# Holding one stream's expert row fetches back to the later long convolutions of a hybrid layer

## The chip, the cores and the metric

The kernel runs on one core of a Trainium2 chip. The metric is device time in microseconds (us), from the start to the end of one execution. The core has five engines that run their own instruction lists in order and wait for each other through semaphores: TensorE (PE in the profile), VectorE (DVE), ScalarE (ACT), GpSimd (POOL) and SyncE (SP), and 16 DMA engines that all of them can give transfers to.

## What is computed

One layer of a model runs over two groups of tokens, a prompt of 256 tokens (stream P) and a sample of 1024 tokens (stream Q), with the same weights. Cut to what matters here:

```python
def trunk_layer(x, cond, h0, p):
    y, final_state = token_mixer(x * (1 + sc1) + sh1, h0, p)   # projection, RG-LRU scans, long convolutions
    x = layer_norm(ALPHA * x + g1 * y, ...)
    y = peer(x * (1 + sc2) + sh2, ...)                         # 8 heads x top 16 of 16384 experts
    x = layer_norm(ALPHA * x + g2 * y, ...)

def peer_block(xb):                       # 128 tokens
    idx, g = route(xb)                    # 128 expert numbers and weights per token
    u = u_tab[idx]                        # one row of 1024 floats per token and expert
    act = gelu(einsum("td,thkd->thk", xb, u))
    v = v_tab[idx]
    return einsum("thk,thkd->td", g * act, v)

def hyena_branch(hy):                     # two rounds of FFT convolution over the whole sequence
    z = x1 * fft_long_conv(v, kf[:, 0], skip[0])
    z = x2 * fft_long_conv(z, kf[:, 1], skip[1])
```

## The kernel before

**The experts of stream P as row fetches.** `experts` (its helper `fetch` stands at L1046) handles a block of 128 tokens with 128 fetches from the u table and then 128 from the v table. A fetch is one indirect DMA that GpSimd issues: 128 rows of 1024 floats, one row per token, 0.52 MB. VectorE then takes the row tile: L1059 multiplies a u row with the token's vector and sums (the vector `h` lies in PSUM), L1068 adds a weighted v row to the sum. Both keep VectorE busy for one instruction per fetch. Five row buffers (`row`, `bufs=5`) go round, so a sixth fetch waits on GpSimd until VectorE has taken the first. P has two blocks, so 512 fetches, numbered 0 to 511 by `fetched`; numbers 256 to 383 are the u rows of the second block. They are filler beside the mixer of stream Q.

**Where they may run.** `PACE["P"]` is a list of (number, mark): a fetch may not stand on GpSimd ahead of the mark of the last entry whose number is not above its own (`paced`). A mark is a GpSimd instruction of stream Q that `mark` noted; `"hy"` counts 32 of them, the products L721 at the end of each long convolution. `_pace(first, (name, start, stop, each), ...)` gives the numbers: each mark lets `each` more fetches through. Fetches ahead of the first number have no mark and go as soon as buffers and GpSimd allow. The rest of the order of all engines is set by the framework's scheduler, which reorders within the dependences.

**The long convolutions of stream Q.** `hyena` runs eight convolutions, two rounds (`o`) over four groups of 256 channels, in pairs: groups 0 and 1 in round 0, then in round 1, then groups 2 and 3. One convolution (`convolve`) is

- folds of the input (L341) and their splits into high and low parts (`oph`, `opl`, L204, L205), on VectorE and GpSimd;
- the analysis: TensorE multiplies the folds with cosine and sine tables for four blocks of frequencies, into two PSUM banks each (L162);
- on VectorE the products with the filter's spectrum (L703, L704, L705, `ya`, `yb`, `k`) and their split (`yh`, `yl`);
- the synthesis: TensorE multiplies `yh` and `yl` back to time, 192 matmuls into four banks, a quarter of them with the last frequency block;
- VectorE takes the four banks in two pairs of sums (L720, `z`), and GpSimd multiplies each by the gate `x` (L721). These four are four `"hy"` marks.

In this text "the first pair" and "the second pair" of a convolution are its L720 instructions, two and two. The numbers 1 to 8 name the convolutions in order. What follows them is branch A and B (`branch`): ScalarE's queue loads the results of the scans and of the convolutions (`z<-d_ZAQ`, `z<-d_ZBQ`, L794), they are split, and the products with `w_branch_a` start.

Of the kernel before, what the change touches and what calls it, by code (L numbers as in the profile page):

```python
# [20 lines left out]
P = 128  # L21
# [31 lines left out]
def _pace(first, *segments):  # L53

    out = []
    for name, start, stop, each in segments:
        for i in range(start, stop):
            out.append((int(first), (name, i)))
            first += each
    return out  # L60
# [1 line left out]

SCANS = (10, 14, 18, 22, 26, 30, 34, 38, 41)
ORDER = (0, 1, 5, 2, 3, 4, 6, 7)
PACE = {"P": _pace(340, ("hy", 0, 32, 0.5), ("w_branch_a", 0, 8, 4), ("w_branch_b", 0, 8, 4), ("w_out", 0, 16, 2), ("query", 0, 32, 2)),
        "Q": _pace(0, ("spread", 16, 80, 3))}


# [32 lines left out]
def body(ctx, tc, A, O):  # L101
# [88 lines left out]
    def paced(pace, i, ins):  # L190

        at = [m for first, m in pace if first <= i]
        if at:
            tc.add_manual_dep(ins.ins, marks[at[-1]].name, mybir.DependencyInfo(mybir.DependencyClass.NoSync, mybir.DependencyReason.DATA), reason="pace")
# [844 lines left out]
    def experts(s, blocks, out, peer, ready=None):  # L1039

        for b in blocks:
            idx, g = s.route[b]

            def fetch(tab, k):
                t = row(peer)
                i = nc.gpsimd.indirect_dma_start(out=t[:], out_offset=None, in_=A[tab],  # L1046
                                                 in_offset=bass.IndirectOffsetOnAxis(ap=idx[:, k:k + 1], axis=0))
                paced(PACE[s.name], fetched[s.name], i)
                fetched[s.name] += 1
# [405 lines left out]
```

## Time and profile before

| | us |
|---|---|
| median of 3 runs (5077.14 to 5094.96) | 5087.09 |
| the profiled execution, its own time | 5079.36 |
| its span | 5077.6 |
| TensorE busy | 4316.5 (85%) |
| VectorE busy | 4128.4 (81%) |
| GpSimd busy | 3045.0 (60%) |
| ScalarE busy | 1821.2 (36%) |

Shares are means over stages with different limits. The projection of stream Q runs until about 1685 us, the eight convolutions from 1697 to about 2140, the branches, output, norm and queries until about 2600, the routing and the spreading of the experts' weights until about 3400, then the dense experts until 4925 and the last row fetches of stream Q to the end. A row of a busy-time view gives a stretch, its length, the busy time of each engine with the number of instructions, the clock that TensorE was granted as a share of 2.4 GHz, the mean busy share of the DMA engines and their GB/s. A row of a timeline gives start, length, engine, line, operation and, in square brackets, how long the engine sat idle before it and what ended that.

### The profile page before, as it was taken

Reading aid. Unit: us, or ns where it says so; the run is one execution under the profiler, and the core shown is the slowest. Engines: PE = TensorE matmul, PEld = TensorE weight load, DVE = VectorE, ACT = ScalarE, POOL = GpSimd, SP = SyncE. Lnnn points to the kernel's source line nnn. Section 1 sums busy time; section 2 is a strip of 40 time slices with the busy share of each in tenths; the row PEclk is TensorE's granted clock in tenths of the full one; section 3 lists DMA queues with packets and bytes.
Section 4 is the critical chain, followed back from the end, with each engine's and each line's share of the span. In section 5 each row is a group of like instructions: output and inputs, shape, how many; then the busy total and the mean of one; then the engine's idle time right before and its main releaser. Section 6 shows DMA issues by size and latency. Waiting matters only on the chain.

```text
span 5077.6 us, 67877 instructions
## 1 busy us (share of the span) xinstructions
PE 4316.5 (85%) x23707; PEld 3762.4 (74%) x23707; DVE 4128.4 (81%) x7106; ACT 1821.2 (36%) x2716; POOL 3045.0 (60%) x2218
## 2 busy tenths in 40 slices
PE   6888788899999678789798888888699999999970
PEld 4666687677777668767587888888588888888860
DVE  6779563989994877466759999999589899989898
ACT  4546333346663112121433544445232222222210
POOL 1456451478886765368664365667467676666765
PEclk8999899999999889999899999999899999999995
DMA  6676646798889853388685478887988999989988
GB/s 210 219 237 201 194 159 220 245 325 305 299 302 328 300 177 119 127 319 300 246 290 180 158 240 281 282 282 261 342 302 327 343 334 340 330 311 338 339 285 296
DMA packets 613378, 1357.26 MB, mean 267 GB/s; under 512 B 64254, under 2 KB 284103, under 8 KB 612524
## 3 DMA queue, kind: packets, MB, share of 16 engines
q1 hardware_dynamic: 417196, 658.69, 38.5%
q0 software_dynamic: 187776, 680.61, 38.0%
q10 hardware_dynamic: 8064, 13.64, 0.7%
q8 instruction: 186, 3.05, 0.2%
q14 instruction: 156, 1.28, 0.1%
HBM read 1182.81 MB, written 169.93 MB: 266 GB/s over the span
## 4 chain that ended last, share of the span: by engine, by line
PE 22%; DVE 16%; issue 7%; DMA 7%; POOL 4%; SPq 2%; ACT 1%; POOLq 0%; ACTq 0%; DVEq 0%
PE bank L162 18%; PE bank L171 3%; DVE row L1059 3%; DVE oa L1098 2%; POOL row L1046 2%; DMA row<-in_peer_v,idxQ 2%; SPq L1104 2%; DVE y L1068 2%; DVE ob L1095 1%; DVE hot L1090 1%; DVE gt L1151 1%; PE bank L1101 1%; DMA row<-in_peer_u,idxQ 1%; DVE S L931 1%; DVE iu L930 1%
## 5 line engine op out<-in xcount | busy, mean ns | idle before, releaser
L1068 DVE SCALAR_TENSOR_TENSOR y<-row,act,y 128x1024 f32<-128x1024 f32 x635 | 815.7, 1285 | 199.6 <-DMA row<-in_peer_v,idxP 112.6
L1059 DVE SCALAR_TENSOR_TENSOR row<-row,h 128x1024 f32<-128x1024 f32 x640 | 763.2, 1212 | 131.7 <-DMA row<-in_peer_u,idxP 67.5
L162 PE MATMUL bank<-hTh,uh 128*128 128x320 f32 x2048 | 646.5, 316 | 46.0 <-ACT uh L204 45.9
L162 PE MATMUL bank<-hTl,uh 128*128 128x320 f32 x2048 | 645.3, 315 | 0.0
L162 PE MATMUL bank<-hTh,ul 128*128 128x320 f32 x2048 | 643.5, 315 | 1.8 <-POOL ul L205 1.8
L1046 POOL DMA_INDIRECT row<-in_peer_u,idxQ x384 | 411.5, 1072 | 293.7 <-DVE row L1059 187.2
L1046 POOL DMA_INDIRECT row<-in_peer_v,idxQ x384 | 411.6, 1072 | 270.5 <-DVE y L1068 202.1
L205 POOL TENSOR_TENSOR wl<-wr,wh 128x1024 fp32r<-128x1024 f32 x148 | 364.3, 2462 | 331.9 <-ACT wh L204 303.9
L162 PE MATMUL bank<-vl,wh 128*128 128x512 f32 x1280 | 497.5, 390 | 3.8 <-DVE vl L205 3.5
L162 PE MATMUL bank<-vh,wh 128*128 128x512 f32 x1280 | 489.2, 392 | 13.0 <-ACT wh L204 7.2
L162 PE MATMUL bank<-vh,wl 128*128 128x512 f32 x1280 | 482.9, 390 | 0.8 <-DVE wl L205 0.6
L162 PEld LDWEIGHTS bank<-hTh,uh 128*128 128x128 f32 x2048 | 394.3, 193 | 48.6 <-ACT uh L204 47.3
L162 PEld LDWEIGHTS bank<-hTl,uh 128*128 128x128 f32 x2048 | 394.4, 193 | 1.2
L162 PEld LDWEIGHTS bank<-hTh,ul 128*128 128x128 f32 x2048 | 393.0, 192 | 2.7 <-POOL ul L205 2.6
L1046 POOL DMA_INDIRECT row<-in_peer_u,idxP x256 | 275.0, 1074 | 142.4 <-DVE row L1059 79.4
L204 ACT ACTIVATE wh<-wr 128x1024 fp32r<-128x1024 f32 x176 | 185.7, 1057 | 443.2 <-issue 171.6
L1046 POOL DMA_INDIRECT row<-in_peer_v,idxP x256 | 277.3, 1083 | 102.3 <-issue 35.6
L205 POOL TENSOR_TENSOR ul<-raw,uh 128x1024 fp32r<-128x1024 f32 x100 | 242.8, 2428 | 111.6 <-ACT uh L204 110.1
L1101 PE MATMUL bank<-ob,oa 128*128 128x128 f32 x1280 | 190.7, 302 | 125.5 <-DVE oa L1098 74.4
L162 PEld LDWEIGHTS bank<-vh,wh 128*128 128x128 f32 x1280 | 240.9, 188 | 67.9 <-ACT wh L204 9.7
L162 PEld LDWEIGHTS bank<-vl,wh 128*128 128x128 f32 x1280 | 240.7, 188 | 53.7 <-DVE vl L205 4.4
L162 PEld LDWEIGHTS bank<-vh,wl 128*128 128x128 f32 x1280 | 240.7, 188 | 52.4 <-DVE wl L205 1.5
(444 smaller groups left out, 12046.6 us busy)
## 6 DMA issues: line engine op xcount, KB each, us to landing
raw<-in_peer_uT SPq DMA_DIRECT2D x128, 512.0 KB
raw<-in_peer_v SPq DMA_DIRECT2D x128, 512.0 KB
wr<-in_w_in SPq DMA_DIRECT2D x112, 512.0 KB
d_GD<-G SPq DMA_DIRECT2D x40, 1024.0 KB
gt<-d_GD SPq DMA_DIRECT2D x128, 320.0 KB
w<-in_w_ada SPq DMA_DIRECT2D x48, 512.0 KB
wr<-in_w_query SPq DMA_DIRECT2D x48, 512.0 KB
d_AD<-a SPq DMA_DIRECT2D x72, 320.0 KB
```

The source lines that it names most:

```text
L162: nc.tensor.matmul(out, l, r, start=(i == 0), stop=(i == len(ops) - 1))
L171: nc.tensor.matmul(out, a, b, start=(i + j == 0), stop=(i == KT - 1 and j == len(ops) - 1))
L204: nc.scalar.activation(hi, src, AF.Copy)
L205: note(eng, eng.tensor_tensor(lo, src, hi.bitcast(F32), op=ALU.subtract))
L930: nc.vector.max_index(iu[:, g, 0:8], v[:, g, 0:8], Sg)
L931: nc.vector.match_replace(S2[:], v[:, g, 0:8], Sg, NEG)
L1046: i = nc.gpsimd.indirect_dma_start(out=t[:], out_offset=None, in_=A[tab], in_offset=bass.IndirectOffsetOnAxis(ap=idx[:, k:k + 1], axis=0))
L1059: nc.vector.scalar_tensor_tensor(t[:], t[:], 1.0, h[:], op0=ALU.mult, op1=ALU.mult, accum_out=act[:, k:k + 1])
L1068: nc.vector.scalar_tensor_tensor(y[:], t[:], act[:, k:k + 1], y[:], op0=ALU.mult, op1=ALU.add)
L1098: nc.vector.tensor_scalar(oa[:, i, :], iota_k[:], tr[:, 0, t:t + 1], tr[:, 2, t:t + 1], op0=ALU.is_equal, op1=ALU.mult)
L1101: nc.tensor.matmul(ps[:, i * P:(i + 1) * P], oa[:, i, :], ob[:, i, :], start=True, stop=True)
L1104: nc.sync.dma_start(GD[j:j + 16, :, b * P:(b + 1) * P].rearrange("j i t -> i j t"), G[:, j:j + 16, :])
```

## The change

`PACE["P"]` gets two other numbers and one more segment:

```diff
-PACE = {"P": _pace(340, ("hy", 0, 32, 0.5), ("w_branch_a", 0, 8, 4), ...
+PACE = {"P": _pace(292, ("hy", 0, 12, 0.5), ("hy", 12, 32, 3), ("w_branch_a", 0, 8, 4), ...
```

Before, fetches 0 to 339 are free and 340 to 355 go one for every two marks of the convolutions. Now 0 to 291 are free, 292 to 297 go one for every two of the marks 0 to 11, and 298 to 357 three for each of the marks 12 to 31. The segments behind follow as they did, with numbers that are two higher (358 stands where 356 stood). No instruction is added or removed.

The instruction lists of the two kernels differ as follows. On VectorE at the end of convolution 1 (`row,act<-row,h` is the taking of a u row, `z<-bank_14370` and `z<-bank_14488` are the two pairs of convolution 1, `ya` and `yb` with bank 14654 and 14667 belong to convolution 2):

```order
-L1059 SCALAR_TENSOR_TENSOR row,act<-row,h 128x1024 x2
+L720 TENSOR_TENSOR z<-bank_14370,ya 128x512 x2
+L720 TENSOR_TENSOR z<-bank_14488,ya 128x512 x2
+L1059 SCALAR_TENSOR_TENSOR row,act<-row,h 128x1024
+L703 TENSOR_TENSOR ya<-bank_14654,k_14680 128x512
+L703 TENSOR_TENSOR ya<-bank_14654,k_14682 128x512
 L704 TENSOR_TENSOR yb<-bank_14667,k_14682 128x512
-L1059 SCALAR_TENSOR_TENSOR row,act<-row,h 128x1024 x3
-L720 TENSOR_TENSOR z<-bank_14370,ya 128x512 x2
```

The rows that stood ahead of the first pair are gone from there. Counted over the whole list, 23 fewer rows stand ahead of the first pair of convolution 1, and 25 fewer between it and the first pair of convolution 2 (2 where there were 27).

On VectorE between convolutions 4 and 5 (bank 15916 and 16026 are the two pairs of convolution 4, and what follows is the analysis of convolution 5):

```order
 L720 TENSOR_TENSOR z<-bank_15916,ya 128x512 x2
+L1059 SCALAR_TENSOR_TENSOR row,act<-row,h 128x1024
 L720 TENSOR_TENSOR z<-bank_16026,ya 128x512 x2
-L1059 SCALAR_TENSOR_TENSOR row,act<-row,h 128x1024
+L1059 SCALAR_TENSOR_TENSOR row,act<-row,h 128x1024 x2
 L704 TENSOR_TENSOR yb<-bank_16257,k_16272 128x512
-L205 TENSOR_TENSOR opl<-fold,oph 128x512
+L205 TENSOR_TENSOR opl<-fold,oph 128x512 x2
+L1059 SCALAR_TENSOR_TENSOR row,act<-row,h 128x1024
```

One row now stands between the two pairs and eleven behind them, in the first half of the next analysis, where there were none and two. It is the same in front of convolutions 6, 7 and 8. Behind convolution 8's second pair 11 rows now stand ahead of the splits of the branch, where there was one.

On GpSimd at the end of convolution 4 (`z<-z,x` is a mark, `row<-in_peer_u` a fetch):

```order
-L721 TENSOR_TENSOR z<-z,x 128x512 x2
-L1046 DMA row<-in_peer_u,idxP_9588 128x1024
-L721 TENSOR_TENSOR z<-z,x 128x512 x2
-L1046 DMA row<-in_peer_u,idxP_9588 128x1024
+L721 TENSOR_TENSOR z<-z,x 128x512
+L1046 DMA row<-in_peer_u,idxP_9588 128x1024 x3
+L721 TENSOR_TENSOR z<-z,x 128x512
+L1046 DMA row<-in_peer_u,idxP_9588 128x1024 x3
+L721 TENSOR_TENSOR z<-z,x 128x512 x2
+L1046 DMA row<-in_peer_u,idxP_9588 128x1024 x2
```

Three fetches stand behind each of the first two marks, and the six of the other two are mixed with the folds and splits that follow.

## Rows read from the trace of the kernel before

**Rows 1.** Page, part 1: busy time, share of the span, instructions.

```profile
PE 4316.5 (85%) x23707; PEld 3762.4 (74%) x23707; DVE 4128.4 (81%) x7106; ACT 1821.2 (36%) x2716; POOL 3045.0 (60%) x2218
```

**Rows 2.** Busy times: from first pair to first pair of the convolutions, and behind.

```profile
core 0: us, PE busy (x) PEld busy (x) DVE busy (x) ACT busy (x) POOL busy (x), PEclk, DMA share, GB/s
1697.00:1775.00 78.00, 52.05 (x353) 49.42 (x354) 74.82 (x113) 15.34 (x26) 59.22 (x52) 0.78 0.87 291
1775.00:1843.00 68.00, 42.95 (x275) 40.08 (x275) 62.55 (x93) 10.13 (x17) 46.59 (x41) 0.77 0.72 250
1843.00:1897.00 54.00, 45.48 (x346) 43.63 (x346) 38.65 (x49) 11.05 (x19) 30.25 (x21) 0.91 0.32 102
1897.00:1942.00 45.00, 40.78 (x329) 40.12 (x328) 27.98 (x40) 10.43 (x17) 24.52 (x18) 0.96 0.32 101
1942.00:1989.00 47.00, 43.45 (x358) 43.01 (x357) 30.63 (x41) 14.93 (x42) 22.89 (x17) 0.96 0.39 129
1989.00:2040.00 51.00, 45.73 (x371) 44.84 (x370) 34.97 (x44) 11.88 (x26) 26.29 (x19) 0.93 0.31 99
2040.00:2088.00 48.00, 40.11 (x316) 39.16 (x315) 33.59 (x42) 10.80 (x19) 26.94 (x19) 0.93 0.29 94
2088.00:2127.00 39.00, 39.00 (x334) 39.00 (x333) 23.27 (x35) 6.25 (x10) 15.86 (x12) 1.00 0.27 82
2127.00:2175.00 48.00, 20.77 (x118) 16.23 (x116) 11.85 (x16) 18.81 (x55) 18.75 (x14) 0.72 0.86 304
```

**Rows 3.** The same for line 1059 alone (two records for each row taken).

```profile
1775.00:1843.00 68.00, 32.52 (x54) 0.77 0.72 250
1942.00:1989.00 47.00, 2.46 (x4) 0.96 0.39 129
```

**Rows 4.** Line 1059 from 1690 to 2140: shortest, median, longest in ns.

```profile
L1059 DVE SCALAR_TENSOR_TENSOR row<-row,h x76: 1203/1211/1223, 1692.1 to 2135.2; 128x1024 f32<-128x1024 f32 x76
```

**Rows 5.** VectorE's timeline at the ends of convolutions 1, 2 and 4 to 8.

```profile
1774.77 1.29 DVE L720 TENSOR_TENSOR z<-bank,ya 128x512 f32<-128x512 f32 x2
...
1844.63 1.29 DVE L720 TENSOR_TENSOR z<-bank,ya 128x512 f32<-128x512 f32 x2 [5.67 <-PE bank L162]
...
1853.92 1.22 DVE L1059 SCALAR_TENSOR_TENSOR row<-row,h 128x1024 f32<-128x1024 f32 x1 [4.66 <-DMA row<-in_peer_u,idxP]
...
1855.07 1.28 DVE L720 TENSOR_TENSOR z<-bank,ya 128x512 f32<-128x512 f32 x2
...
1941.95 1.29 DVE L720 TENSOR_TENSOR z<-bank,ya 128x512 f32<-128x512 f32 x2 [8.48 <-ACT ya L715]
1948.90 1.29 DVE L720 TENSOR_TENSOR z<-bank,ya 128x512 f32<-128x512 f32 x2 [5.66 <-ACT ya L715]
...
1989.45 1.29 DVE L720 TENSOR_TENSOR z<-bank,ya 128x512 f32<-128x512 f32 x2 [9.34 <-PE bank L162]
...
2040.16 1.29 DVE L720 TENSOR_TENSOR z<-bank,ya 128x512 f32<-128x512 f32 x2 [8.36 <-ACT ya L715]
...
2088.01 1.29 DVE L720 TENSOR_TENSOR z<-bank,ya 128x512 f32<-128x512 f32 x2 [7.41 <-ACT ya L715]
...
2126.76 1.29 DVE L720 TENSOR_TENSOR z<-bank,ya 128x512 f32<-128x512 f32 x2 [5.92 <-ACT ya L715]
```

**Rows 6.** GpSimd's timeline behind the first pair of convolution 2.

```profile
1845.40 2.54 POOL L721 TENSOR_TENSOR z<-z,x 128x512 f32<-128x512 f32 x2 [9.06 <-DVE z L720]
1848.09 1.42 POOL L1046 DMA_INDIRECT row<-in_peer_u,idxP  x1 [0.15 <-issue]
```

**Rows 7.** The chain that ended last, behind the convolutions: start, us, what.

```profile
2170.33 12.13 DMA z<-d_ZBQ
```

**Rows 8.** TensorE's timeline: matmuls at the higher and at the lower clock.

```profile
1942.47 0.28 PE L162 MATMUL bank<-yh,kN 128*128 128x256 f32 x1
1942.59 0.28 PE L162 MATMUL bank<-yl,kN 128*128 128x256 f32 x1
...
1974.62 0.41 PE L162 MATMUL bank<-yh,kN 128*128 128x256 f32 x1
1974.84 0.41 PE L162 MATMUL bank<-yl,kN 128*128 128x256 f32 x1
```

**Rows 9.** Busy times of the stage of routing and spreading.

```profile
2600.00:3400.00 800.00, 683.45 (x4358) 649.10 (x4357) 766.61 (x2427) 356.48 (x450) 448.59 (x314) 0.94 0.72 237
```

More of the change, by code (lines that the diff above doesn't have):

```diff
@@ L64 @@
 ORDER = (0, 1, 5, 2, 3, 4, 6, 7)
-PACE = {"P": _pace(340, ("hy", 0, 32, 0.5), ("w_branch_a", 0, 8, 4), ("w_branch_b", 0, 8, 4), ("w_out", 0, 16, 2), ("query", 0, 32, 2)),
+PACE = {"P": _pace(292, ("hy", 0, 12, 0.5), ("hy", 12, 32, 3), ("w_branch_a", 0, 8, 4), ("w_branch_b", 0, 8, 4), ("w_out", 0, 16, 2), ("query", 0, 32, 2)),
         "Q": _pace(0, ("spread", 16, 80, 3))}
```

## The prediction, made before the changed kernel ran

> **What bounds the kernel now.** I read the page's busy shares first: TensorE 85% and VectorE 81% [rows 1], so neither alone explains the span, and each stage has to be read by itself. All that the change moves lies in one stage, so next comes the view of busy time cut at the first pair of each long convolution [rows 2]. The reader is to see two kinds of stretch. In the first two (78 and 68 us) VectorE is idle for only 3.2 and 5.5 us and TensorE is granted 0.78 and 0.77 of its clock: VectorE is the bound. In the six others VectorE is idle 14 to 17 us each, and the clock is 0.91 to 1.00. The same view for line 1059 alone [rows 3] says what fills the first kind: 27 rows take 32.5 us of the second stretch, while a later stretch has 2 rows. A row costs 1.21 us whatever runs beside it, 1203 to 1223 ns over 76 of them [rows 4].
>
> Then VectorE's timeline [rows 5] shows where the idle time of a later convolution lies: 5.9 to 9.3 us ahead of the first pair and some 5.7 us between the pairs, while TensorE finishes the synthesis. The analysis between them is one unbroken run of VectorE work. So a row costs nothing in the end of a synthesis and its full price in an analysis. Everything behind the convolutions needs their output, and the later stages keep their work, so a shift of their end should pass to the end of the program.
>
> **Part 1, rows taken out of convolutions 1 and 2.** 23 rows fewer stand ahead of the first pair of convolution 1: 23 x 1.21 = 27.8 us of VectorE. That pair, at 1774.77, waited for nothing [rows 5]; without filler a wait for TensorE comes back, 5.7 to 9.3 us. I take 7: gain 20.8. Convolution 2 loses 25 rows, 30.3 us; its idle time grows from 5.5 us to the 15.6 us that is the mean of the stretches of 5 to 8 (16.4, 16.0, 14.4, 15.7 [rows 2]): gain 20.2. Its second pair also waited behind a row whose transfer had not landed, and came 10.44 us after the first, against 6.95 in convolution 4 [rows 5]. That gives up to 3.5 us; some other work was done in that gap, so I take 2. Sum of part 1: 43 us. The ends: 60 if no wait comes back, 39 if the longest does and the last gain is nothing.
>
> **Part 2, rows put ahead of convolutions 5 to 8.** Each now gets 12 rows instead of 2. The order shows where: one between the pairs, eleven behind them, in the first half of the next analysis, where VectorE has no gap. That is 9 rows more at 1.21 = 10.9 us in the run that sets the pace. The row between the pairs is not free either: its fetch is issued behind the first mark. In convolution 2 the fetch stood behind two marks and the second pair came 10.44 us after the first; one mark is half of 2.54 us [rows 6], so now it comes 10.44 - 1.27 = 9.2 us after, 2.2 later than the 6.95 of a pair without a row. Sum per convolution 13.1, for four 52.4. Some comes back: TensorE has work in hand when the analysis ends, so the wait ahead of the first pair can shrink, at best to the 5.67 us of the loaded convolution 2, from 9.34, 8.36, 7.41 and 5.92 [rows 5]: 8.3 us in all. Since the rows stand in the first half, and TensorE meets an unchanged second half, I take half of it: 4.2. Part 2 costs 48 us. The ends: if the gaps shrink to the 5.5 us of the loaded convolution 2, 10.1 of 12.1 us is hidden each time and four cost 8 us; at full price and with the clock of the rival below, 71.
>
> **Part 3, rows behind convolution 8.** Eleven rows stand there where one stood; 10 more fetches of 0.52 MB are 5.2 MB. The chain there is the loading of the branch's operands, a 12.1 us stretch of it among others [rows 7], and the DMA engines are 86% busy at 304 GB/s [rows 2], so 5.2 MB at 304/0.86 = 353 GB/s take 14.8 us. About half of the fetches are issued ahead of the last marks, when the engines have room. I take half, 7.4, between 0 (all land ahead of the loads) and 14.8. The Trainium skill, "DMA: Bandwidth & Descriptors", section on issuing engines not being separate queues, says that transfers of every issuing queue run on the same 16 engines and interleave; no row here shows a fetch beside these loads, and by that rule alone the term would be its upper end and the sum 7 us more. VectorE's eleven rows are no term of their own: VectorE is idle there for 36 of 48 us [rows 2].
>
> **Part 4, two rows fewer later.** P's fetches end two earlier, in a stage where VectorE is busy 767 of 800 us [rows 9]: 2 x 1.21 = 2.4 us gained, or nothing. GpSimd's own issue work is the same in total; it is hidden since GpSimd is at most 60% busy in the later stretches [rows 2].
>
> **Sum.** -43 + 48 + 7.4 - 2.4 = +10 us on the profiled execution's 5079.4 us, 5089 us. The median of the runs lies 7.7 us above that execution, so I put the forecast at 5087 + 10 = 5097 us: the saving of the first two convolutions is given back in the last four, and a bit more at the branch.
>
> **Rivals.** First, faster: the rows find the gaps. In convolution 2, 27 rows left only 5.5 us idle, so VectorE can be packed when rows are at hand. For it speaks that each later stretch has 14 to 17 us free for 12.1 us of new work; against it, that in convolution 2 rows went whenever a buffer came free, and here they come in bursts behind the marks, into the busy half. Part 2 is then 8: -43 + 8 + 7 - 2 = -30, 5057 us.
>
> Second, slower: TensorE's clock falls in convolutions 5 to 8. The mechanism is one: the eleven rows make TensorE wait for VectorE in every analysis, the granted clock drops as in convolutions 1 and 2 (0.77), and the last quarter of the synthesis, 48 matmuls that need the last product, runs at the lower level. Matmuls start 0.12 us apart at the higher and 0.22 at the lower level [rows 8], so 48 of them take 4.6 us longer, 18 us for four convolutions, and no wait shrinks. Part 2 is then 71 and, with the branch's upper end, the sum is -43 + 71 + 15 - 2 = +41, 5128 us. It decides from about 1.3 us per convolution on, since the forecast is only 5 us below the bound of slower. For it speaks that the lower level already appears inside convolution 5 [rows 8]; against it, that this stretch kept 0.96 [rows 2]. The Trainium skill, "TensorE: Matmul & The Clock Gate", section on HAM oscillation, says that a wait which returns in every pass of a loop throttles the clock in every pass. By that rule this rival is the forecast; the trace agrees in convolutions 1 and 2 and not yet in the later ones.
>
> Third, the change does nothing: the end of the convolutions is not what the branch waits for, since its weights and loads bound it anyway. Then 5087 us. Against it: the chain runs through the last marks and the loads behind them.
>
> **How the numbers follow.** About 0.3% (15 us) is what a measurement of this kernel can tell from no change. The forecast has 0.38 and the third rival 0.06, both within the bound: same 0.44. The faster rival has 0.20, the slower 0.36, because the forecast stands near the upper bound and its two unproven terms (clock, loads) both point up. The likeliest case alone reaches from 5083 (more of the wait shrinks, no price at the branch) to 5110. The range for 8 in 10 takes in both rivals' sides, 5058 to 5126.
>
> **What would show it.** Cut at the first pairs, convolution 1's end should come 21 us earlier after its start, convolution 2 should last about 48 us, and 5 to 8 about 59, 63, 60 and 51, each 12 us longer. If those last four grow by 5 us or less, the first rival holds; if the granted clock there falls below 0.9, the second. The second pair of convolutions 4 to 7 should come some 9 us after the first, behind a row that waited for its transfer. The time from the last mark to the first steady products of branch A should grow by 0 to 15 us. The forecast is wrong if the later stages differ by more than their start, since the order of routing and spreading moved a little too.

## The result and the profile after

The changed kernel takes 5131.2 us (median of 6 runs, 5123.1 to 5134.7); the kernel before, beside it, 5081.4. The ratio is 1.0093, with a 95% interval of 1.0081 to 1.0105: some 47 us slower. By the medians it is 49.8 us. The forecast was 5097 (5058 to 5126): the trade between the convolutions came out nearly as forecast, the end did not. The profiled execution of after took 5124.3 us, its span is 5122.4, 44.8 us more than that of before.

Page, part 1, of after (against [rows 1]):

```profile
PE 4342.7 (85%) x23707; PEld 3789.0 (74%) x23707; DVE 4126.2 (81%) x7106; ACT 1821.3 (36%) x2716; POOL 3050.1 (60%) x2218
```

The instructions are the same; TensorE's 26 us more go with a mean granted clock of 0.919 against 0.926. Next the busy times of after, cut at its own first pairs (columns as in [rows 2]): convolution 1's end, convolution 2, convolutions 5 to 8, and from the last mark to the branch's steady products.

```profile
core 0: us, PE busy (x) PEld busy (x) DVE busy (x) ACT busy (x) POOL busy (x), PEclk, DMA share, GB/s
1698.70:1757.20 58.50, 44.14 (x287) 42.36 (x288) 47.60 (x63) 14.12 (x24) 32.17 (x24) 0.77 0.47 159
1757.20:1807.70 50.50, 45.08 (x353) 44.31 (x353) 32.54 (x44) 10.81 (x18) 25.80 (x19) 0.90 0.28 90
1904.50:1963.10 58.60, 48.61 (x354) 47.10 (x354) 42.45 (x61) 13.78 (x34) 32.10 (x27) 0.85 0.53 184
1963.10:2023.90 60.80, 44.46 (x350) 43.88 (x349) 45.33 (x63) 13.24 (x35) 34.13 (x29) 0.86 0.51 178
2023.90:2082.20 58.30, 45.72 (x340) 44.12 (x340) 44.71 (x63) 10.69 (x18) 34.73 (x29) 0.82 0.49 167
2082.20:2131.20 49.00, 44.46 (x345) 43.42 (x344) 33.94 (x55) 6.91 (x14) 25.13 (x22) 0.93 0.51 178
2145.20:2225.50 80.30, 33.22 (x113) 23.83 (x113) 45.81 (x48) 23.45 (x48) 42.48 (x35) 0.64 0.75 280
```

Convolution 2 now lasts 50.5 us, where it lasted some 70 [rows 2, 5], and VectorE has 18 us free in it. Convolutions 5 to 8 last 58.6, 60.8, 58.3 and 49.0; their first pairs stood 47.5, 50.7, 47.9 and 38.8 us apart before [rows 5]. VectorE's timeline of after shows both sides: the waits ahead of the first pairs that came back in convolutions 1 and 2, and the row that stands between the pairs of convolution 4 and waits 6.2 us for its transfer.

```profile
1757.21 1.29 DVE L720 TENSOR_TENSOR z<-bank,ya 128x512 f32<-128x512 f32 x2 [7.43 <-ACT ya L715]
...
1807.69 1.29 DVE L720 TENSOR_TENSOR z<-bank,ya 128x512 f32<-128x512 f32 x2 [8.11 <-ACT ya L715]
...
1904.52 1.29 DVE L720 TENSOR_TENSOR z<-bank,ya 128x512 f32<-128x512 f32 x2 [8.99 <-ACT ya L715]
1912.00 1.22 DVE L1059 SCALAR_TENSOR_TENSOR row<-row,h 128x1024 f32<-128x1024 f32 x1 [6.20 <-DMA row<-in_peer_u,idxP]
...
1913.15 1.28 DVE L720 TENSOR_TENSOR z<-bank,ya 128x512 f32<-128x512 f32 x2
```

Where the 45 us lie is best seen from five points that both traces have. The table gives how much later than in the kernel before each is reached, in us, counted from the first matmul of the convolutions (which starts at 1695 to 1713 us in all these executions, so that the start is taken out). "Branch" is the last L802 (VectorE's last product of the branches' first stage), "spread" the first L1101 (TensorE's first matmul of the spreading), "dense" the first L1151 (VectorE's first weighting of the dense experts). The medians are those of all runs; in brackets the median of the kernel before beside it. A single profiled execution can lie up to 15 us from its kernel's median, so ends are compared by medians, places by profiles. In before the queries run to 2763 us, the spreading's last matmul starts at 3546 and the dense experts begin at 3619: the stages lie later than the rough times given ahead of the prediction.

| run | last mark | branch | spread | dense | end | median of runs |
|---|---|---|---|---|---|---|
| after | 7.2 | 17.4 | 13.5 | 37.3 | 45.1 | 5131.2 (5081.4) |
| e1 | 1.8 | 3.4 | -2.3 | 8.6 | 11.6 | 5101.6 (5084.6) |
| e2 | 9.8 | 8.3 | 5.3 | 12.1 | 1.8 | 5082.2 (5084.6) |
| e3 | 43.9 | 56.8 | 45.6 | 55.2 | 44.2 | 5129.8 (5084.6) |
| e4 | -38.2 | -33.8 | -11.5 | 11.6 | 5.3 | 5087.0 (5084.6) |
| e5 | 9.1 | 11.1 | 16.0 | 29.1 | 21.1 | 5099.4 (5081.7) |
| e6 | 3.7 | -6.7 | 3.3 | 1.1 | -9.0 | 5075.5 (5081.7) |
| e7 | 14.9 | 23.7 | 15.8 | 25.4 | 21.4 | 5101.1 (5081.7) |
| e8 | -0.1 | -2.0 | -1.6 | 5.5 | -0.4 | 5081.5 (5081.7) |
| e9 | 17.1 | 25.8 | 15.9 | 40.5 | 32.4 | 5106.2 (5081.4) |
| e10 | 13.7 | 17.7 | 20.2 | 32.0 | 36.4 | 5116.2 (5081.4) |
| e11 | -39.3 | -41.3 | -43.4 | -11.3 | 2.9 | 5081.6 (5081.4) |
| e12 | -24.2 | -34.0 | -27.8 | -17.0 | -20.4 | 5057.7 (5081.4) |
| e13 | 7.4 | 22.2 | 22.2 | 35.5 | 29.9 | 5113.0 (5084.2) |
| e14 | 10.2 | 20.8 | 22.4 | 49.5 | 55.8 | 5129.1 (5084.2) |
| e15 | 2.9 | -1.3 | -2.1 | 25.0 | 28.6 | 5109.6 (5084.2) |
| e16 | -24.3 | -25.8 | -28.8 | -23.1 | -18.3 | 5064.8 (5084.2) |

In after, 7.2 us are lost by the last mark and 10.2 in the branch. Output and queries give 3.9 back, the stage from the first spreading to the dense experts loses 23.8, the rest 7.8. The last 28 us lie in stages whose work the change does not touch, but for two rows fewer. A difference of 3 to 5 us between two places is within what two executions of the same orders show (after, e13 and e14 up to the branch).

### The profile page after: what moved, and what is told of

Its sections match the earlier page's. It is cut to its first block, busy times and chain, and to the rows that moved or that the text cites. A ratio compares the mean times of both kernels' runs of the same rounds, so it can differ in the third digit from the quotient of the medians.

```text
span 5122.4 us, 67888 instructions
## 1 busy us (share of the span) xinstructions
PE 4342.7 (85%) x23707; PEld 3789.0 (74%) x23707; DVE 4126.2 (81%) x7106; ACT 1821.3 (36%) x2716; POOL 3050.1 (60%) x2218
## 3 DMA queue, kind: packets, MB, share of 16 engines
q1 hardware_dynamic: 417196, 658.69, 38.2%
## 4 chain that ended last, share of the span: by engine, by line
PE 21%; DVE 18%; DMA 7%; issue 6%; POOL 4%; SPq 2%; ACT 1%; POOLq 0%; DVEq 0%; ACTq 0%
PE bank L162 18%; DVE oa L1098 3%; PE bank L171 3%; DVE row L1059 3%; POOL row L1046 2%; DVE y L1068 2%; DMA row<-in_peer_v,idxQ 2%; SPq L1104 2%; DVE ob L1095 1%; DVE hot L1090 1%; DMA row<-in_peer_u,idxQ 1%; DVE gt L1151 1%; DMA row<-in_peer_v,idxP 1%; DVE iu L930 1%; DVE S L931 1%
## 5 line engine op out<-in xcount | busy, mean ns | idle before, releaser
L162 PE MATMUL bank<-vh,wh 128*128 128x512 f32 x1280 | 488.6, 392 | 21.1 <-DVE acc L1141 11.4
L1101 PE MATMUL bank<-ob,oa 128*128 128x128 f32 x1280 | 194.6, 304 | 137.9 <-DVE oa L1098 84.7
L1101 PEld LDWEIGHTS bank<-ob,oa 128*128 128x128 f32 x1280 | 177.8, 212 | 152.1 <-ACT G L1102 51.3
```

The costliest lines, as they stand in the source:

```text
L162: nc.tensor.matmul(out, l, r, start=(i == 0), stop=(i == len(ops) - 1))
L1101: nc.tensor.matmul(ps[:, i * P:(i + 1) * P], oa[:, i, :], ob[:, i, :], start=True, stop=True)
```

## The experiments

In the expectations, "the planner" is the framework's scheduler.

### Part 2 alone (e3) and part 1 alone (e4)

```diff
# e3
+_pace(340, ("hy", 0, 12, 0.5), ("hy", 12, 32, 3), ("w_branch_a", 0, 8, 4), ...
# e4
+_pace(292, ("hy", 0, 32, 0.5), ("w_branch_a", 0, 8, 5), ("w_branch_b", 0, 8, 5), ("w_out", 0, 16, 3), ("query", 0, 32, 2.5))
```

> Part 2 alone: the first number is 340 as before, and three fetches go per mark from mark 12 on; the numbers behind stand 50 higher. Theory A: first pairs of convolutions 1 to 4 as before to 2 us; convolutions 5 to 8 last 58, 61, 58 and 49 us as in the changed kernel, 42 us more than before, so that the last mark comes near 2138 + 45 = 2183; the branch 13 us longer. Behind it 50 rows fewer are left, at 1.21 us each up to 60 us less in the stage of routing and spreading, where VectorE is the bound: end between 5076 and 5136. If instead the convolutions 5 to 8 are longer in the changed kernel only because their start came early, they last 48, 51, 48 and 39 us here. Theory B adds up to 25 us either way behind the branch and says nothing of the convolutions.

Measured: 5129.8 us, ratio 1.0088 (1.0068 to 1.0108). Busy times of e3, convolutions 5 to 8:

```profile
1946.20:2005.70 59.50, 48.79 (x351) 47.53 (x351) 43.02 (x61) 13.78 (x34) 32.10 (x27) 0.83 0.54 182
2005.70:2067.20 61.50, 45.52 (x348) 44.76 (x347) 45.28 (x63) 13.24 (x34) 33.87 (x29) 0.81 0.52 176
2067.20:2123.00 55.80, 45.88 (x342) 44.18 (x342) 41.48 (x64) 10.71 (x18) 36.19 (x29) 0.85 0.50 175
2123.00:2171.30 48.30, 44.02 (x351) 43.01 (x351) 34.18 (x45) 9.42 (x20) 25.79 (x22) 0.93 0.55 186
```

They are as long as in after, though their start came no earlier: the rows make them long, 40 us in all. The branch is 12.9 us longer. The 50 rows that are missing later gave back 11 us at most: 56.8 us behind at the branch, 55.2 at the dense experts, 44.2 at the end.

> Part 1 alone: fetches from 292 on are held, one goes for every two marks through all eight convolutions as before, and the 48 held fetches follow behind: five per mark in place of four in branches A and B, three in place of two in the output projection, and two and a half in place of two in the queries. Theory A: convolutions 1 and 2 gain 37 us as in the changed kernel, nothing is lost in 5 to 8, so the last mark comes near 2101. Behind it 48 rows at 1.21 to 1.29 us are 60 us of VectorE; all at full price the end is 5081 - 37 + 60 = 5104, all hidden 5044, half 5074. Theory B: the same convolutions, and 25 us either way behind the branch.

Measured: 5087.0 us, ratio 1.0003 (0.9989 to 1.0017). The last mark comes 38.2 us earlier, so the gain of part 1 is whole without part 2. It is given back: 4.4 us in the branches and 22 in output projection and queries, where the rows went, and 23 from the first spreading to the dense experts, where by the marks none of them went.

### The place of the rows within a convolution (e7)

```diff
-("hy", 12, 32, 3)
+("hy", 12, 15, 0), ("hy", 15, 16, 12), ("hy", 16, 19, 0), ("hy", 19, 20, 12), ...
```

> The changed kernel with the twelve fetches of each of convolutions 4 to 8 released together, behind its fourth mark, in place of three behind each mark. So no row stands between the two pairs any more. The prediction put 2.2 us of each convolution's 13.1 on the second pair that waits for such a row. Theory A: the second pair comes 6.9 us after the first (8.2 to 8.6 in the changed kernel), convolutions 5 to 8 are 1 to 2 us shorter each, 5 us in all, and the row work of 11 us each stays. If the place of the rows matters more (released later, they go into the later half of the analysis, or a burst of fetches lands later), the convolutions are longer, by up to 5 us each. At the branch twelve fetches now stand behind the last mark, in place of nine: 2 to 6 us later.

Measured: 5101.1 us, ratio 1.0033 (1.0019 to 1.0048). In convolution 4 the second pair comes 6.95 us after the first again; in after it came 8.63 behind it:

```profile
1898.71 1.29 DVE L720 TENSOR_TENSOR z<-bank,ya 128x512 f32<-128x512 f32 x2 [9.57 <-ACT ya L715]
1905.66 1.29 DVE L720 TENSOR_TENSOR z<-bank,ya 128x512 f32<-128x512 f32 x2 [5.66 <-ACT ya L715]
```

So the row between the pairs cost 1.7 us. The convolutions are longer all the same (61.3, 63.6, 64.8 and 51.6 us): the second alternative of the expectation holds. Convolution 7 grew by 6.5 us against after, more than the 5 that were allowed. That the end was 30 us earlier than after's is not due to the convolutions, which had lost 8 us more by the last mark, nor to the branch (8.8 us longer than before).

### The branch: which engine splits (e5, e6)

```diff
# e5 on after, e6 on before
-split_into(op[k][t0][0], lo, lo.bitcast(F32), elt(0.5))
+split_into(op[k][t0][0], lo, lo.bitcast(F32), (elt(0.5), nc.vector)[1])
```

In after one split on VectorE lasts as long as twelve on GpSimd. VectorE's splits of z in after (shortest, median, longest in ns):

```profile
L205 DVE TENSOR_TENSOR z<-z x16: 675/680/13766, 2172.7 to 2215.6; 128x512 fp32r<-128x512 f32 x16
```

GpSimd's timeline of after beside it, and the entry in the chain that ended last:

```profile
2185.91 14.75 POOL L205 TENSOR_TENSOR z<-z 128x512 fp32r<-128x512 f32 x12
```

```profile
2187.45 13.78 DVE z L205
```

> The changed kernel with one edit at the branch: the second parts of the z splits of line 795, which go in turn to GpSimd and VectorE, all go to VectorE. In the changed kernel one such split of 0.68 us took 13.8 us on VectorE beside 12 splits in a row on GpSimd, and TensorE waited some 15 us there for VectorE's splits. Theory A (that hold-up is 8 of the 13 us that the branch lost, and the fetches that delay the loads of z are the other 5): first pairs of the convolutions as in the changed kernel to 3 us; the time from the last mark to the last product of branch A's and B's first stage (line 802's last) falls from 244.6 us to about 237, against 234.4 before; no split longer than 3 us. Theory B (fetches and loads alone make the branch late): the branch stays at 244 us. Behind the branch the order is laid out anew again; if that matters by tens of us, the later stages move by 10 us or more from those of the changed kernel, in either direction; if not, the end is 5131 - 8 = 5123.

> The kernel before with the same edit at the branch as in the run above. In the kernel before a split was held up too, for 15.8 us, but TensorE waited under 1 us for VectorE there. Theory A: nothing to gain at the branch, last mark to line 802's last within 3 us of 234.4; the end at 5081 but for what the new order behind brings. If the hold-up costs time in this kernel too, the branch is 5 to 8 us shorter.

Measured: e5 5099.4 us, ratio 1.0037 (1.0024 to 1.0050); e6 5075.5 us, ratio 0.9990 (0.9976 to 1.0004). The splits of e5:

```profile
L205 DVE TENSOR_TENSOR z<-z x32: 676/687/3092, 2173.1 to 2211.9; 128x512 fp32r<-128x512 f32 x32
```

From the last mark to the last L802, e5 takes 236.4 us where after takes 244.6, as expected. But e6 takes 224.0 where before takes 234.4: theory A fell there. On before the gain is clear: the five other runs with its splits and its fetches beside them (e2, e8, e11, e15, e16) take 230 to 233 us, and e12, which has the edit, 224.5. At the end it is not: e6's interval takes in 1. On after the gain is not shown by e5 alone, since the runs with the changed pattern and the old splits scatter from 236.0 (e1) to 249.2 (e13). The edit also takes away GpSimd's slower splits, so the hold-up's own share stays open. So the old splits cost time without the change too and are not shown to be what it made worse, although the profile of before shows TensorE waiting less than 1 us for VectorE's. What the change made worse are the loads ahead of them, which ScalarE issues (only SyncE, ScalarE and GpSimd issue transfers in these traces). The last mark in GpSimd's timeline, in before (the second of the two, at 2138.32) and in after:

```profile
2137.10 2.49 POOL L721 TENSOR_TENSOR z<-z,x 128x512 f32<-128x512 f32 x2 [5.89 <-DVE z L720]
```

```profile
2145.24 1.27 POOL L721 TENSOR_TENSOR z<-z,x 128x512 f32<-128x512 f32 x1 [2.16 <-DMA x<-d_HYQ]
```

ScalarE's first split of a loaded z, in its timeline of before:

```profile
2159.89 0.63 ACT L204 ACTIVATE z<-z 128x512 fp32r<-128x512 f32 x1 [17.42 <-DMA z<-d_ZAQ]
```

And of after:

```profile
2172.00 0.63 ACT L204 ACTIVATE z<-z 128x512 fp32r<-128x512 f32 x1 [22.14 <-DMA z<-d_ZAQ]
```

That is 21.6 us behind the last mark in before, with one fetch behind it, and 26.8 in after, with six. It is 24.2 with five (e1) and 32.5 with twelve (e7), and in all 18 kernels 19.9 to 21.8 with one and 25.6 to 27.2 with six: about 1 us for each fetch behind the last mark. The other half of the 10.2 us goes with the order of splits and products behind the loads, which no run moves alone: VectorE's last z split comes 58.8 us behind the mark in before, 70.4 in after.

### The numbers behind the convolutions (e1, e2, e8)

```diff
# e1: after, with 356 behind the convolutions as before
-("hy", 12, 32, 3)
+("hy", 12, 32, 2.9)
# e2: before, with 358 behind the convolutions as in after
-_pace(340, ("hy", 0, 32, 0.5), ...
+_pace(340, ("hy", 0, 32, 0.5625), ...
# e8: before
-_pace(340, ...
+_pace(342, ...
```

> The changed kernel with 2.9 in place of 3 fetches per mark, so that 356 stands again where 358 stood and the marks behind the convolutions carry the numbers they had before. Theory A (the rows themselves cost the time: 37 us gained in convolutions 1 and 2, 42 lost in 5 to 8, some 13 at the branch, and the rest is what the shift by two brings): convolutions as in the changed kernel, last mark near 2145, and the end near 5081 + 18 = 5099 us, since the shift is undone. Theory B (the planner lays out everything behind the convolutions anew for any difference ahead of it, and the new layouts differ by tens of us): convolutions as in the changed kernel to 3 us, but the stages behind the branch differ again from both kernels, by 10 us or more in at least one of them, and the end lies anywhere from 5070 to 5130. Theory C (the rows moved late load something that is still felt in the dense stage): same end as the changed kernel, 5131 to 5 us.

> The kernel before with 0.5625 in place of 0.5 fetches per mark in the convolutions: two fetches more there in all, and the numbers behind stand two higher, as in the changed kernel; nothing is held in convolutions 1 and 2. Theory A: two rows more, 2.4 us, two fewer later: 5081 to 5 us. If the shift by two itself cost the 27 us behind the branch: 5081 + 27 = 5108. Theory B: first pairs of the convolutions within 3 us of before, and the stages behind the branch moved by 10 us or more in one direction or the other; the end between 5060 and 5110.

> The kernel before with 342 in place of 340: two fetches more are free, everything behind stands two numbers higher, and nothing is held or bunched. A change with next to no work in it. Theory A: first pairs within 3 us of before, the end at 5081 to 5 us. Theory B (every difference lays the later stages out anew, and that alone is worth tens of us): at least one of the stages behind the branch (output projection, routing, spreading, dense) differs by 10 us or more from before, and the end by 5 to 25 us either way.

Measured: e1 5101.6 us, ratio 1.0027 (1.0014 to 1.0040); e2 5082.2, 0.9995 (0.9983 to 1.0008); e8 5081.5, 1.0000 (0.9986 to 1.0014). e1 has the convolutions of after to 6 us and ends 30 us earlier, near theory A's 5099. But the shift by two is not the cause: e2 and e8 have it on before and cost nothing, and e7, with 358 as in after, ends as early as e1. Theory C fell with e1. The scatter of theory B does not show in the ends of e2 and e8. e2's last mark came 9.8 us late, where both theories allowed 3, and nothing of that is left at the end: a shift of the convolutions does not simply pass through.

### The pattern of the change at other numbers (e9, e10)

```diff
-_pace(292, ("hy", 0, 12, 0.5), ("hy", 12, 32, 3), ...
+_pace(290, ...   # e9
+_pace(294, ...   # e10
```

> The changed kernel with 290 in place of 292 as first number: two fetches more are held, all later numbers two lower, the pattern of the change unchanged. Theory A (the 47 us are what the displaced rows cost): the end within 5 us of the changed kernel's 5131. Theory B (rows cost some 17 us, as in the three variants of the changed kernel that ended at 5099 to 5102, and the other 30 us belong to the one order that the planner found for the changed kernel): the end between 5090 and 5112, with the convolutions as in the changed kernel to 5 us and the difference behind them.

> The changed kernel with 294 in place of 292: two fetches fewer are held, all later numbers two higher. Theory A: within 5 us of 5131. Theory B: between 5090 and 5112, as for the run above; both together say whether 5131 or 5100 is what the pattern of the change is worth.

Measured: e9 5106.2 us, ratio 1.0045 (1.0031 to 1.0060); e10 5116.2, 1.0068 (1.0045 to 1.0092), 4 us above theory B's bound and 10 below theory A's. The last marks lie 9.9 and 6.5 us behind after's, where 5 was expected. With e1 and e7, four kernels of the same pattern lie between 5101 and 5116, and the changed kernel lies above all of them, though e10's interval still touches after's.

### The order behind the branch alone (e13, e14, e15)

```diff
# e13 on after, e15 on before
-("w_out", 0, 16, 2)
+("w_out", 0, 16, 2.1)
# e14 on after
-("query", 0, 32, 2)
+("query", 0, 32, 2.05)
```

> The changed kernel with 2.1 in place of 2 fetches per mark of the output projection: its lists are word for word the changed kernel's up to the output projection, and differ in over 2000 lines of TensorE's and VectorE's lists behind it. Theory A (the displaced rows cost the 47 us): 5131 to 5 us. Theory B (15 to 30 us of them belong to the one order behind the branch): convolutions and branch as in the changed kernel, line 802's last 17 us behind the kernel before, and the end between 5095 and 5117.

> A control: the changed kernel with 2.05 in place of 2 fetches per mark of the queries, which leaves TensorE's list as it is and changes 301 lines of VectorE's. Both theories: 5131 to 7 us. If it moves as far as the run above, a moved row matters by itself and not the order that the planner makes of it.

> The kernel before with the same edit at the output projection, 2.1 in place of 2, after which some 2700 lines of TensorE's list differ. Theory A: 5081 to 5 us. Theory B: a new order, with a stage behind the output projection 10 us or more away from before, and the end between 5065 and 5105; together with the earlier small edits of the kernel before (5082 and 5082) it tells how far such orders scatter.

Measured: e13 5113.0 us, ratio 1.0058 (1.0037 to 1.0079); e14 5129.1, 1.0085 (1.0064 to 1.0106); e15 5109.6, 1.0055 (1.0036 to 1.0074). Up to the branch e13 and e14 are after, and e15 is before, within 5 us (table). One or two fetches let through earlier in the output projection take 18 us from after and add 25 to before, 5 more than theory B allowed. The control, where TensorE's order is after's throughout its trace, stays with after. TensorE's order in e13 parts from after's only at the first spreading (2776 us), that of e15 from before's at 2748. So the order that the scheduler lays out from there on is worth some 20 us by itself. The whole stage from the first spreading to the dense experts, as busy times, first in before, then in after, then in e15, e13 and e14:

```profile
2762.90:3619.20 856.30, 696.42 (x4665) 679.58 (x4665) 794.97 (x2102) 383.82 (x474) 491.90 (x358) 0.91 0.76 251
```

```profile
2776.10:3656.20 880.10, 703.59 (x4681) 686.79 (x4679) 803.08 (x2098) 383.12 (x475) 499.17 (x357) 0.90 0.74 244
```

```profile
2760.40:3643.80 883.40, 704.22 (x4670) 686.86 (x4670) 810.87 (x2098) 382.45 (x474) 495.01 (x357) 0.91 0.74 244
```

```profile
2788.00:3657.60 869.60, 696.00 (x4678) 680.52 (x4678) 791.88 (x2101) 382.63 (x474) 496.51 (x361) 0.91 0.75 250
```

```profile
2791.90:3675.30 883.40, 705.94 (x4681) 689.55 (x4679) 808.90 (x2098) 384.55 (x476) 500.69 (x357) 0.90 0.74 243
```

Every engine's work in after and e15 is that of before within 2%, and the stage is 24 to 27 us longer. What differs is how the routing (up to the last L954) and the spreading's 320 pieces (L1098) are interleaved. The pieces that are left behind the routing (count, then shortest, median, longest in ns), again in before, after and e15:

```profile
L1098 DVE TENSOR_SCALAR oa<-iota_k,tr x108: 331/336/3136, 3304.9 to 3538.5; 128x128 f32<-128x128 f32 x108
```

```profile
L1098 DVE TENSOR_SCALAR oa<-iota_k,tr x120: 330/336/4378, 3313.7 to 3566.2; 128x128 f32<-128x128 f32 x120
```

```profile
L1098 DVE TENSOR_SCALAR oa<-iota_k,tr x120: 331/339/4370, 3304.4 to 3555.9; 128x128 f32<-128x128 f32 x120
```

Only before and e6 leave 108 and take 854 to 856 us for the stage; after and all the others of e1 to e10 and e13 to e15, but for e4 with its late routing, leave 116 or 120 and take 863 to 883. So some 10 us of the 24 go with the 12 pieces that the order of before has ahead of the routing's end. They need not reach the end: e2 and e8 leave 120 too, take 863 us, and end level with before, their dense experts and tail being 10 and 6 us shorter. Why after, e9, e14 and e15 take 10 to 20 us more than the rest with the same number is not settled, nor is after's 7.8 us in the dense stage and the tail, which e14 shows too (6.3) and e13 does not (-5.6).

### A version that beats both (e11, e12, e16)

```diff
# e11
+_pace(292, ("hy", 0, 32, 0.5), ..., ("w_out", 0, 16, 2), ("query", 0, 32, 3.5))
# e16; e12 is the same with the edit of e5
+_pace(316, ("hy", 0, 32, 0.5), ..., ("w_out", 0, 16, 2), ("query", 0, 32, 2.75))
```

> Part 1 of the change, and the 48 held fetches all go to the queries, three and a half for each mark in place of two; convolutions 3 to 8, branches and output projection have as many as before. In the run that held them for all later stages alike, 16 rows cost some 5 us in the branches, 12 in the output projection and 10 in the queries. Theory A, by that: last mark 38 us earlier, kept through branch and output projection, and the queries, where VectorE is busy 228 of 295 us, take 48 rows for 20 to 35 us: end at 5081 - 38 + 28 = 5071, between 5060 and 5085. If rows cost their full 1.29 us in the queries: 5081 - 38 + 62 = 5105. If the fetches do not fit beside the loads there (71% of the DMA time is taken, 25 MB more at 240/0.71 = 338 GB/s are 74 us of it): up to 5115.

> Two things that cost little: half of the 48 fetches are held (first number 316) and go to the queries (2.75 per mark), and the branch's splits all go to VectorE, as in an earlier run. Theory A: convolutions 1 and 2 gain 18 us, the queries lose 8 to 14, the splits bring up to 10: end between 5058 and 5076, below both kernels. Theory B: the same convolutions, but the new order behind them takes the gain away or doubles it: 5050 to 5095.

> Half of the 48 fetches held (first number 316) and given to the queries at 2.75 per mark, without the edit at the branch's splits. The version with both ended at 5058. If the half-held rows are what gained: 5058 to 7 us, the convolutions 24 us earlier and kept to the end. If the splits did: 5070 to 5080, with the branch some 7 us longer from the last mark to line 802's last.

Measured: e11 5081.6 us, ratio 1.0000 (0.9986 to 1.0013); e16 5064.8, 0.9957 (0.9942 to 0.9973); e12 5057.7, 0.9948 (0.9930 to 0.9967). Busy times of the queries of before, then of convolution 2 and the queries of e16:

```profile
2468.10:2762.90 294.80, 241.12 (x1183) 203.05 (x1183) 228.18 (x683) 106.81 (x182) 163.98 (x102) 0.91 0.71 240
```

```profile
1789.70:1835.10 45.40, 38.92 (x301) 37.71 (x301) 36.97 (x47) 9.95 (x17) 27.28 (x19) 0.89 0.33 99
...
2458.50:2748.40 289.90, 242.09 (x1212) 204.36 (x1212) 233.29 (x647) 104.33 (x180) 187.50 (x126) 0.91 0.81 281
```

The 24 held rows free convolution 2 of 24 us, and the queries, where VectorE has 57 to 67 us idle, take them without growing. Of e16's gain some 18 to 22 us are left at the end. In e11 the queries take 48 rows as easily (43.4 us ahead at the first spreading), but the stage from there to the dense experts lasts 888 us, 32 more than in before, and dense experts and tail 14 more: the gain is gone, and theory A's 5071 was 10 us too low. VectorE's last routing comes 702 us after the first spreading there, against 537 in before; no run shows that this alone is the cause. The splits' part in e12 (7 us against e16) lies inside the two intervals, though the branch is 8 us shorter.

## Why the prediction was wrong, step by step

**Part 1** was right: 17.3, 19.4 and 1.0 us for convolutions 1, 2 and 3 against 20.8, 20.2 and 2; 37.7 against 43. The waits of 7.4 and 8.1 us came back; 7 was taken for the first.

**Part 2** was right: 11.1, 10.1, 10.5 and 10.2 us, 41.9 in all, against 48. Ten rows more are 12.1 us of VectorE, and nearly all of it came out as length, as e3 shows alone. The second pairs came 1.3 to 1.8 us later, not 2.2, and the waits ahead of the first pairs shrank by 4.5 us, where 4.2 were taken. The faster rival falls: none of the four grew by less than 10 us.

**The sign named for the slower rival was a bad one.** The granted clock fell from 0.96, 0.93, 0.93 and 1.00 to 0.85, 0.86, 0.82 and 0.93, in three of the four below the 0.9 that was to prove it, and the time did not follow: the four cost 42 us, not 71. The rule of the Trainium skill on the returning wait ("TensorE: Matmul & The Clock Gate", HAM oscillation), weighed in the prediction, agrees with the clock here. The price that the rival put on it is not seen: the four grew by 10.1 to 11.1 us each, less than the 12.1 of the ten rows on VectorE, for which TensorE waits some 36 us in the four, 13 in before.

**Part 3** was in its bounds: 10.2 us against 7.4 (0 to 14.8). About half is the later landing of the loads, as argued. The other half, the order of splits and products behind them, was not in the sum. e13, whose orders are after's up to there, shows 14.8, so the size is known to some 5 us only. The third rival falls here: 7.2 us at the last mark are 17.4 behind the branch, and e4's 38.2 are 33.8.

**Part 4 is the step that failed**: two rows less, 2.4 us gained; measured is a loss of 27.7 from the branch to the end. Behind it stands the sentence that the later stages keep their work, so that a shift should pass to the end. They kept their work and not their order. The prediction named a difference in the later stages as what would make it wrong, and gave it no term and no width. e13 and e15 show that a new order there is worth -18 and +25 us with next to nothing else changed. Which feature of the order costs the time stays open. Up to the branch the sum had 12.4 us (-43 + 48 + 7.4), and the trace shows 17.4. By medians the seven kernels with the changed pattern and the old splits (e1, e7, e9, e13, e10, e14, after) end 17, 19, 25, 29, 35, 45 and 50 us above before beside them, and three with the pattern of before (e2, e8, e15) at -2, 0 and +25. So the sum up to the branch describes the lowest of the seven, and up to 30 us of after's 47 go with its own order. That e1 and e7 end near the 17 us is no proof of the sum: they have their own orders too.

## What to carry to other kernels

Where a scheduler lays out the order, an edit also buys a new order of everything behind it: give that a term of its own, of the size that edits of one or two fetches show on the same kernel (here -2, 0 and +25 us on before, -2 to -25 on the changed kernel), and judge an idea by several kernels of its pattern, not by one. Filler work cost nearly its full price where its engine set the pace (10 to 11 of 12.1 us), whatever the idle time of that stage added up to. It was free in a stage where its engine had room: 24 rows in the queries kept their gain to the end, 48 did not.

## What the runs showed of the hardware

A split of 0.68 us on VectorE lasted 13.8 us in after (15.8 in before) while GpSimd ran twelve splits back to back, one every 1.23 us, and ended 0.55 us behind the last of them. With all splits on VectorE the longest was 3.1 us in e5. The Trainium skill, "SBUF — State Buffer", section "SBUF: two separate sides", says that an operation of VectorE with two inputs in SBUF and one of GpSimd that reads SBUF lock each other out for a whole instruction. The traces agree, and at this place VectorE was not let in between GpSimd's instructions either: the price was the whole run. It is not so everywhere. In convolution 3 of before GpSimd runs four instructions back to back from 1875.80 to 1881.95, and VectorE's split among them, with two inputs in SBUF as well, ends 0.55 us behind the second:

```profile
1875.80 2.77 POOL L205 TENSOR_TENSOR opl<-fold,oph 128x512 fp32r<-128x512 f32 x2 [1.35 <-ACT oph L204]
1878.53 1.72 POOL L205 TENSOR_TENSOR yl<-ya,yh 128x512 fp32r<-128x512 f32 x1
1880.21 1.74 POOL L341 TENSOR_TENSOR fold<-v 128x512 f32<-128x512 f32 x1
```

```profile
1877.32 1.80 DVE L205 TENSOR_TENSOR opl<-fold,oph 128x512 fp32r<-128x512 f32 x1
```

What decides between the two is not settled.
